# Four feed-forward stages whose operands share eight blocks of SBUF, first evictions that go to the result's place, and a reordered last column block

## The chip, the cores and the metric

The kernel runs on one core of a Trainium2 chip as one program. The metric is the device time of one execution in microseconds (us); three runs of the kernel before are shown. Engines are named as in the profile: PE is the matrix engine and PEld its weight loads, DVE the vector engine, ACT the scalar engine, POOL GpSimd, SP the engine that only issues transfers. A row such as "L298" names line 298 of the kernel before; the order listings of the changed kernel carry its own line numbers, about 20 higher.

## The reference, cut to what matters

Two blocks of two layers each work on x of 512 tokens by 1024 features in float32. Each layer has a mixer (forgetting attention, HGRN2, stick-breaking attention with pooling, gated linear attention) and then a feed-forward part of width 2816. The change touches the four feed-forward parts and the norms in front of them:

```python
def swiglu_ffn(h, w_in, w_out):                      # layers 0 and 1
    gate, up = jnp.split(jnp.einsum('bsd,df->bsf', h, w_in), 2, axis=-1)
    return jnp.einsum('bsf,fd->bsd', jax.nn.silu(gate) * up, w_out)

def conv_ffn(h, w_up, conv_w, conv_b, w_down):       # layers 2 and 3
    u = h @ w_up
    up = jnp.pad(u, ((0, 0), (CONV_WIDTH - 1, 0), (0, 0)))
    conv = conv_b
    for j in range(CONV_WIDTH):
        conv = conv + conv_w[j] * up[:, j:j + s]
    a, g = jnp.split(conv, 2, axis=-1)
    return (jax.nn.silu(a) * g) @ w_down
```

In front of each stands rms_norm(h, gain).

## The kernel before, in words

**Numbers.** A float32 operand is held as a high part (fp32r) and a low part; a product is three matmuls (`mm3`, L296). Making the parts is a "split": a cast on ACT and a subtraction on DVE (L148 and L149 for activations, L201 and L202 for weights).

**The up product.** The four feed-forward stages are called F0 to F3 here (`plan_up` tags up0 to up3). The product with w_up is a Winograd scheme over 2x2 quadrants: seven products p = 1 to 7 in place of eight, for each of 11 column blocks j of 256 columns of each half. The left operands of the seven (`LEFT`, L751) are made by `combine` (L415) from the normed activation: a11 and a12 from the first half of the tokens, then s1 = a22-a21, s4, s2, s3 = a11-a21 and a22. They lie in pool "xc" (L105), each 8 KB a partition. The sum y that `combine` works in lies above it in pool "y". The right operands are weights, loaded by SP into raw buffers, to which POOL adds other quadrants with accumulating transfers (L166, L204), and split into weight slots W0 to W3. So one raw buffer serves three products in turn: p5, then p6, then p4 (and p3, then p7), with an accumulating transfer between them.

**Order.** `up_order` (L677) sets PE's order: first (j, 1) and (j, 2) for j = 0 to 3 (`up_first`, run while the second half of the norm is still under way), then the rest. From j = 4 each block runs (j,5), (j+1,1), (j,3), (j,6), (j+1,2), (j,7), (j,4). A product is 24 matmuls of 256 columns. PE follows the program's order (`in_order`); DVE, ACT and POOL take the order that the Tile scheduler gives them, and each runs its own queue strictly in that order.

**Evictions.** p5 and then p3 accumulate in one PSUM bank z, and p6 and then p7 in the bank of p1. So p5 has to be copied out before p3 may add to z, and p6 before p7. `swiglu_evac` (L821) copies p5 to a temporary "p5" (L837) and p6 to "u" (L840) in pool "upt"; `conv_evac` (L855) copies them straight to hid (L878, L880), and for j = 0 and 1 POOL copies the gate half from its early buffer c to "g" (L876) in "upt". Pool "upt" lies where y lay.

**The down product.** hid (22 tiles of 512) is split into the resident region R of eight blocks, a tail, and, for tiles 0 and 1, the weight slot W3 (`hidden_at`, L665), and multiplied with w_down (`down`, L922; `out_gemm`, L520). R moves to the other side of SBUF in each feed-forward stage: `ffn_up` (L899) closes the old R, opens W3, hid and three more raw buffers there, and once the up product stands in the program closes xc and opens the new R over it.

A pool's tile that takes the place of an older tile waits for the older one's last use. `high_priority` tells the scheduler to place instructions ahead of others that are ready.

## Time and profile before

| | us |
|---|---|
| median of 3 runs | 2666.98 (2663.35 to 2672.43) |
| the profiled execution, its own time | 2667.84 |
| span of its instructions | 2666.1 |
| PE busy | 2502.1 (94%) |
| DVE busy | 1516.6 (57%) |
| ACT busy | 1173.9 (44%) |
| POOL busy | 660.9 (25%) |
| mean granted TensorE clock | 0.972 of full |

Busy shares are averages over the whole program. PE is the engine that is nearly always busy, so what can be saved is read from its idle time, place by place. A granted clock of 1.00 is 2.4 GHz and 0.50 is 1.2 GHz; a stretch with a mean in between held both.

### The profile page before, as it was taken

To read this page: it belongs to the slowest core of one execution; us is meant where nothing else is said; L and a number is where in the kernel's file an instruction comes from. 1 tells how busy PE (TensorE), PEld (TensorE's weight loads), DVE (VectorE), ACT (ScalarE), POOL (GpSimd) and SP (SyncE) were. 2 spreads that over 40 slices of the span, in tenths; PEclk is the share of its full clock that TensorE was granted. 3 is DMA by queue.
4 is the path that set the end of the run, shared out by engine and by line. 5 is a ranking of instruction groups with operands and counts; after the bars stand their busy time and mean duration, and the time that the engine had idled before them with its cause. 6 is when DMAs were issued, how large, how long until landed. Compare 5 with 4: busy or idle time off the path is not lost. (4 is left out here: it accounts for less than half of the span.)

```text
span 2666.1 us, 40655 instructions
## 1 busy us (share of the span) xinstructions
PE 2502.1 (94%) x16381; PEld 2219.3 (83%) x16381; DVE 1516.6 (57%) x2338; ACT 1173.9 (44%) x1920; POOL 660.9 (25%) x578
## 2 busy tenths in 40 slices
PE   8999889999999998999998998799899999889899
PEld 6677889988898988999897678799687778889778
DVE  5666565552555556655526766677623445677741
ACT  4445445543232234554424543565523333456541
POOL 0000243311321114333024124354112001444300
PEclk9999999999999999999999999899899999999999
DMA  4223279953122124998322116788331224778531
GB/s 131 74 66 100 72 147 191 173 119 123 48 66 70 56 80 111 182 182 159 123 80 71 56 56 132 154 171 150 98 111 50 64 72 130 152 150 171 121 123 40
DMA packets 302776, 294.92 MB, mean 111 GB/s; under 512 B 11581, under 2 KB 292763, under 8 KB 302587
## 3 DMA queue, kind: packets, MB, share of 16 engines
q1 hardware_dynamic: 208123, 195.47, 23.7%
q0 software_dynamic: 94384, 96.81, 23.5%
q8 instruction: 129, 2.11, 0.3%
q14 instruction: 60, 0.49, 0.1%
q10 hardware_dynamic: 80, 0.03, 0.0%
HBM read 290.15 MB, written 2.13 MB: 110 GB/s over the span
## 5 line engine op out<-in xcount | busy, mean ns | idle before, releaser
L202 DVE TENSOR_TENSOR W<-raw,W 128x1024 fp32r<-128x1024 f32 x436 | 551.6, 1269 | 504.6 <-ACT W L201 501.0
L201 ACT CAST W<-raw 128x1024 fp32r<-128x1024 f32 x455 | 472.3, 1041 | 657.3 <-PE g L298 315.0
L298 PE MATMUL g<-R,W 128*128 128x512 f32 (+2 forms) x3096 | 696.5, 373 | 16.5 <-ACT R L148 15.0
L298 PEld LDWEIGHTS g<-R,W 128*128 128x128 f32 (+1 forms) x3096 | 512.9, 191 | 109.5 <-ACT R L148 16.5
L298 PE MATMUL g<-s,W 128*128 128x256 f32 x3840 | 492.4, 288 | 69.5 <-ACT hid L878 22.3
L298 PEld LDWEIGHTS g<-s,W 128*128 128x128 f32 x3840 | 479.9, 195 | 75.4 <-ACT hid L878 25.3
L298 PE MATMUL g<-W,R 128*128 128x256 f32 (+1 forms) x1224 | 235.1, 338 | 0.0
L298 PEld LDWEIGHTS g<-W,R 128*128 128x128 f32 x1224 | 182.1, 192 | 25.9 <-issue 7.4
L298 PE MATMUL a<-a,W 128*128 128x256 f32 x1536 | 197.8, 285 | 0.3 <-POOL a L149 0.3
L298 PEld LDWEIGHTS a<-a,W 128*128 128x128 f32 x1536 | 190.4, 191 | 0.4 <-POOL a L149 0.4
L204 POOL DMA_DIRECT2D raw<-in_ffn_w_in_dram x80 | 106.5, 1374 | 206.4 <-DVE W L202 198.2
L204 POOL DMA_DIRECT2D raw<-in_ffn_w_up_dram x80 | 109.0, 1493 | 88.4 <-DVE W L202 80.7
L298 PE MATMUL g<-a,W 128*128 128x256 f32 x864 | 111.5, 285 | 4.2 <-DVE a L149 4.2
L298 PEld LDWEIGHTS g<-a,W 128*128 128x128 f32 x864 | 107.2, 192 | 5.1 <-DVE a L149 5.1
L298 PE MATMUL g<-R,R 128*128 128x256 f32 (+1 forms) x792 | 105.3, 288 | 0.7 <-ACT y L596 0.7
L298 PEld LDWEIGHTS g<-R,R 128*128 128x128 f32 x792 | 99.4, 192 | 2.7 <-ACT y L596 1.1
L895 POOL TENSOR_TENSOR hid<-u,s 128x512 f32<-128x512 f32 x44 | 70.3, 1608 | 121.9 <-ACT s L892 114.2
L298 PE MATMUL g<-R,X 128*128 128x256 f32 (+1 forms) x528 | 94.0, 333 | 0.0
L202 DVE TENSOR_TENSOR X<-raw,X 128x1024 fp32r<-128x1024 f32 (+1 forms) x39 | 41.1, 1060 | 85.2 <-ACT X L201 85.2
L298 PEld LDWEIGHTS g<-R,X 128*128 128x128 f32 x528 | 80.6, 190 | 9.8
L201 ACT CAST X<-raw 128x1024 fp32r<-128x1024 f32 (+1 forms) x46 | 42.8, 937 | 100.6 <-PE g L298 72.5
L355 POOL TENSOR_TENSOR acc<-acc,sq 128x512 f32<-128x512 f32 x19 | 28.2, 1483 | 233.2 <-ACT sq L354 233.0
(404 smaller groups left out, 3539.0 us busy)
## 6 DMA issues: line engine op xcount, KB each, us to landing
raw<-in_ffn_w_in_dram POOLq DMA_DIRECT2D x88, 512.0 KB, 6.1
raw<-in_ffn_w_up_dram POOLq DMA_DIRECT2D x88, 512.0 KB, 6.3
raw<-in_ffn_w_in_dram SPq DMA_DIRECT2D x74, 512.0 KB, 4.6
raw<-in_ffn_w_up_dram SPq DMA_DIRECT2D x74, 512.0 KB, 4.4
raw<-in_ffn_w_out_dram SPq DMA_DIRECT2D x40, 512.0 KB, 3.5
raw<-in_ffn_w_down_dram SPq DMA_DIRECT2D x40, 512.0 KB, 3.6
raw<-in_hgrn_w_in_dram SPq DMA_DIRECT2D x32, 512.0 KB, 4.1
raw<-in_fox_w_in_dram SPq DMA_DIRECT2D x24, 512.0 KB, 3.8
```

What stands on the lines that cost most here:

```text
L201: nc.scalar.copy(hi, raw)
L202: (nc.gpsimd if s.early else nc.vector).tensor_sub(lo, raw, hi.bitcast(F32))
L204: nc.gpsimd.dma_start(raw.rearrange("p (k c) -> p k c", k=s.nk), s.add, accum_op=ALU.add)
L298: self.nc.tensor.matmul(*args, **kw, **(dict(skip_group_check=True) if skip else {}))
L355: eng.tensor_add(acc[:, cols], acc[:, cols], sq[:, :n])
L895: nc.gpsimd.tensor_mul(hid[:, t], u, s)
```

## The change

1. **Blocks.** One pool of eight blocks of 8 KB stands on a side; its tenants take a block one after the other. On the side of xc, block 0 holds the first half of y (ya), then W3, then R0; blocks 1 to 7 hold a11, a12, s1, s4, s2, s3, a22, then R1 to R7. The second half of y (yb) stands above. hid starts where W3 stood. `hidden_at` fills R in the order 1, 2, 3, 4, 0, 5, 6, 7, and the tail holds six tiles in place of four; W3 no longer holds hid's first two.
2. **Evictions.** `swiglu_evac` copies p5 and p6 to their place in hid; z is added in a step of its own (p == 3) once p3 and p6 are both done. The gate's part for j = 0 and 1 moves from p5 to p7.
3. **combine** runs at high priority, and its POOL steps (two or four L149, two L450) go to DVE.
4. **Order.** The last seven products of blocks 9 and 10 are reordered, and the last (10, 7) gets a load and an accumulating transfer of its own.

```diff
+        self.open_blocks(self.other_side())
+        pool, close = self.open_pool("y", self.other_side())
+        y = Rows(self.blocks(0, "ya", [P, 4, S], F32), pool.tile([P, 4, S], F32, tag="yb", name="yb"))
+        self.xc = {n: self.blocks(1 + i, n) for i, n in enumerate(("a11", "a12", "s1", "s4", "s2", "s3", "a22"))}
...
-            self.combine(pool, work, half, gain, R)
+            with self.tc.high_priority(400):
+                self.combine(pool, work, half, gain, R)
...
-            nc.gpsimd.tensor_sub(a21[i], a11[i], a21[i])
-        for i in range(2):
+            nc.vector.tensor_sub(a21[i], a11[i], a21[i])
             put("s3", g[i], a21[i])
         for i in range(2):
-            put("a22", g[i], a22[i], nc.gpsimd)
+            put("a22", g[i], a22[i])
...
-        if t < 2:
-            return self.slot_at["W3"], t
-        if t >= 18:
-            return self.tail, t - 18
-        k = t - 2 if self.r_side == "left" else t % 16
-        return self.R[k // 2], k % 2
+        if t >= 16:
+            return self.tail, t - 16
+        return self.R[(1, 2, 3, 4, 0, 5, 6, 7)[t // 2]], t % 2
...
+        y, z = n - 2, n - 1
+        rest += [(y, 5), (z, 1), (y, 3), (y, 6), (z, 2), (z, 5), (y, 7), (y, 4), (z, 6), (z, 3), (z, 7), (z, 4)]
...
             elif p == 5:
-                kept[j, "p5"] = new("p5")
-                nc.scalar.copy(kept[j, "p5"], ps)
+                nc.scalar.copy(out[1], two(ps))
             elif p == 6:
-                u = new("u")
-                nc.scalar.copy(u, ps)
-                nc.vector.tensor_add(u, other, u)
-                nc.vector.tensor_mul(out[0], two(u), two(kept.pop((j, "g"))))
+                nc.scalar.copy(out[0], two(ps))
+            elif p == 3:
+                nc.vector.tensor_add(out[0], two(ps), out[0])
...
-        wp, self.close_w3 = self.open_pool("w3", side)
-        self.slot_at["W3"] = wp.tile([P, 2048], F32R, tag="W3", name="W3")
+        self.slot_at["W3"] = self.blocks(0, "W3")
```

Three places show how the instructions move. **POOL at the start of F2** (names with in_ffn_w_up_dram are accumulating transfers; raw_92 and raw_93 serve (0, 5) and (1, 5), the next two numbers above 14900 (before) or 14850 (now) (2, 5) and (3, 5)). Before:

```order
L166 DMA raw_93<-in_ffn_w_up_dram 128x4x256
L367 TENSOR_TENSOR r<-v,mhalf 128x2
L149 TENSOR_TENSOR a_14198<-y,a_14198 128x2x256 x2
L204 DMA raw_92<-in_ffn_w_up_dram 128x4x256
L450 TENSOR_TENSOR y<-y 128x2x256 x2
L876 COPY g<-c_14730 128x2x256
L876 COPY g<-c_14783 128x2x256
L166 DMA raw_14909<-in_ffn_w_up_dram 128x4x256
L204 DMA raw_93<-in_ffn_w_up_dram 128x4x256
L166 DMA raw_14910<-in_ffn_w_up_dram 128x4x256
L204 DMA raw_14908<-in_ffn_w_up_dram 128x4x256
```

Now:

```order
L186 DMA raw_93<-in_ffn_w_up_dram 128x4x256
L387 TENSOR_TENSOR r<-v,mhalf 128x2
L224 DMA raw_92<-in_ffn_w_up_dram 128x4x256
L186 DMA raw_14851<-in_ffn_w_up_dram 128x4x256
L186 DMA raw_14852<-in_ffn_w_up_dram 128x4x256
L224 DMA raw_93<-in_ffn_w_up_dram 128x4x256
L224 DMA raw_14850<-in_ffn_w_up_dram 128x4x256
L901 COPY g<-c_14675 128x2x256
L901 COPY g<-c_14728 128x2x256
L224 DMA raw_91<-in_ffn_w_up_dram 128x4x256
L224 DMA raw_92<-in_ffn_w_up_dram 128x4x256
```

The four POOL steps of combine are gone, and four transfers now stand ahead of the two copies of g instead of behind them.

**DVE at the start of F2**, from the weight split of (0, 5) on (in the change L464 and L467 are the sums, L473 is a11-a21, L169 the low half of an activation's split, L222 that of a weight). Before:

```order
L202 TENSOR_TENSOR W_90<-raw_92,W_90 128x1024
L441 TENSOR_TENSOR sums<-y 128x512 x2
L779 TENSOR_TENSOR c_14783<-a,c_14783 128x512
L149 TENSOR_TENSOR s_14194<-sums,s_14194 128x2x256 x2
L444 TENSOR_TENSOR sums<-sums,y 128x512 x2
L149 TENSOR_TENSOR s_14197<-y,s_14197 128x2x256
L445 TENSOR_TENSOR y<-sums,y 128x2x256 x2
L152 SCALAR_TENSOR_TENSOR s_14195<-sums,s_14195 128x2x256
L149 TENSOR_TENSOR s_14197<-y,s_14197 128x2x256
L152 SCALAR_TENSOR_TENSOR s_14195<-sums,s_14195 128x2x256
L149 TENSOR_TENSOR s_14196<-y,s_14196 128x2x256 x2
L202 TENSOR_TENSOR W_88<-raw_93,W_88 128x1024
```

Now:

```order
L222 TENSOR_TENSOR W_90<-raw_92,W_90 128x1024
L464 TENSOR_TENSOR sums<-yb,ya 128x512
L169 TENSOR_TENSOR a_14147<-yb,a_14147 128x2x256
L464 TENSOR_TENSOR sums<-yb,ya 128x512
L169 TENSOR_TENSOR a_14147<-yb,a_14147 128x2x256
L473 TENSOR_TENSOR ya<-ya 128x2x256
L802 TENSOR_TENSOR c_14728<-a,c_14728 128x512
L169 TENSOR_TENSOR s_14143<-sums,s_14143 128x2x256
L473 TENSOR_TENSOR ya<-ya 128x2x256
L169 TENSOR_TENSOR s_14143<-sums,s_14143 128x2x256
L169 TENSOR_TENSOR s_14146<-ya,s_14146 128x2x256
L467 TENSOR_TENSOR sums<-sums,ya 128x512 x2
```

DVE has the two splits of a22 and the two differences a11-a21 in addition, and no weight split stands among them.

**PE at the end of F2's up product**: a11 to a22 and s1 to s4 are the left operands (14194 before and 14143 now is s1), g<-R and g<-W_14900,W the down product. Before:

```order
L298 MATMUL g<-s_14197,W_89 128x256 x24
L298 MATMUL a<-a_14198,W_14900 128x256 x24
L298 MATMUL g<-s_14194,W_90 128x256 x24
L298 MATMUL g<-s_14196,W_88 128x256 x24
L298 MATMUL g<-s_14195,W_89 128x256 x24
L298 MATMUL g<-s_14197,W_90 128x256 x24
L298 MATMUL a<-a_14198,W_88 128x256 x24
L298 MATMUL g<-W_14900,W_89 128x512 x12
L298 MATMUL g<-R_17143,W_89 128x512 x12
L298 MATMUL g<-R_17144,W_90 128x512 x12
```

Now:

```order
L318 MATMUL g<-s_14143,W_89 128x256 x24
L318 MATMUL g<-s_14146,W_14842 128x256 x24
L318 MATMUL a<-a_14147,W_90 128x256 x24
L318 MATMUL g<-s_14145,W_88 128x256 x24
L318 MATMUL g<-s_14144,W_89 128x256 x24
L318 MATMUL g<-s_14146,W_90 128x256 x24
L318 MATMUL a<-a_14147,W_88 128x256 x24
L318 MATMUL g<-R_17078,W_89 128x512 x12
L318 MATMUL g<-R_17079,W_89 128x512 x12
L318 MATMUL g<-R_17080,W_90 128x512 x12
```

(10, 5) has moved up by two products, (10, 6) stands ahead of (10, 3), and the down product begins from R and not from W3. **DVE there**, before:

```order
L863 SCALAR_TENSOR_TENSOR s<-g,ccol,s 128x511
L864 SCALAR_TENSOR_TENSOR u<-hid,ccol,u 128x510
L863 SCALAR_TENSOR_TENSOR s<-g,ccol,s 128x511
L864 SCALAR_TENSOR_TENSOR s<-g,ccol,s 128x510 x2
L149 TENSOR_TENSOR R_17143<-hid,R_17143 128x2x256 x2
L149 TENSOR_TENSOR R_17144<-hid,R_17144 128x2x256 x2
L149 TENSOR_TENSOR R_17145<-hid,R_17145 128x2x256 x2
```

Now:

```order
L222 TENSOR_TENSOR W_88<-raw_91,W_88 128x1024
L169 TENSOR_TENSOR R_17079<-hid,R_17079 128x2x256 x2
L222 TENSOR_TENSOR W_89<-raw_93,W_89 128x1024
L169 TENSOR_TENSOR R_17080<-hid,R_17080 128x2x256 x2
L169 TENSOR_TENSOR R_17077<-hid,R_17077 128x2x256 x2
L913 TENSOR_TENSOR g<-a,g 128x2x256
L888 SCALAR_TENSOR_TENSOR u<-hid,ccol,u 128x511 x2
L889 SCALAR_TENSOR_TENSOR u<-hid,ccol,u 128x510
L222 TENSOR_TENSOR W_90<-raw_14852,W_90 128x1024
L889 SCALAR_TENSOR_TENSOR u<-hid,ccol,u 128x510
```

The splits of hid into R, which stood behind the whole convolution (L863 and L864), now stand among the last weight splits.

## Rows read from the trace of the kernel before

**Rows 1.** Waits of PE, whole span: who for whom, us in total, times, longest.

```profile
PE g L298 <- ACT hid L878: 22.3, 15, 4.5
PE g L298 <- ACT R L148: 19.6, 7, 6.2
PE g L298 <- ACT hid L880: 18.7, 4, 7.9
```

**Rows 2.** By stretch: length, busy PE, PEld, DVE, ACT, POOL, clock, DMA share; F0, F1.

```profile
356.00:381.00 25.00, 16.55 (x102) 16.14 (x101) 17.23 (x20) 11.25 (x18) 13.07 (x9) 0.80 0.92 143
552.00:576.00 24.00, 19.66 (x142) 18.06 (x142) 14.48 (x18) 13.32 (x20) 3.06 (x2) 1.00 0.58 140
1062.00:1087.00 25.00, 16.51 (x113) 16.11 (x112) 17.44 (x21) 12.48 (x19) 13.19 (x9) 0.86 0.91 141
1257.00:1282.00 25.00, 20.66 (x139) 19.14 (x139) 14.07 (x18) 12.90 (x19) 3.06 (x2) 0.93 0.55 134
```

**Rows 3.** The same view, start and end of F2 and of F3.

```profile
1642.00:1683.00 41.00, 29.12 (x201) 28.09 (x200) 19.07 (x22) 15.69 (x21) 15.96 (x10) 0.83 0.74 143
...
1864.00:1902.00 38.00, 26.00 (x150) 23.22 (x149) 26.91 (x35) 23.10 (x36) 8.76 (x7) 0.82 0.39 93
2298.00:2324.00 26.00, 15.09 (x105) 14.47 (x105) 10.88 (x10) 11.13 (x14) 6.73 (x5) 0.80 0.96 193
...
2500.00:2538.00 38.00, 25.74 (x157) 23.03 (x157) 27.48 (x35) 23.00 (x36) 9.40 (x7) 0.87 0.42 96
```

**Rows 4.** The same view: the steady middle of F0's up product.

```profile
400.00:500.00 100.00, 100.00 (x844) 100.00 (x843) 57.70 (x60) 51.39 (x65) 34.42 (x25) 1.00 0.97 185
```

**Rows 5.** Timeline of PE at F0's start: start, us, what, idle before and releaser.

```profile
360.65 7.36 PE L298 MATMUL m<-s,W 128*128 128x256 f32 x47 [4.15 <-DVE s L149]
372.30 8.72 PE L298 MATMUL m<-s,W 128*128 128x256 f32 x48 [4.29 <-ACT p L837]
```

**Rows 6.** Timeline of DVE there.

```profile
352.74 1.74 DVE L441 TENSOR_TENSOR sums<-y 128x512 f32<-128x512 f32 x2
...
370.94 0.68 DVE L149 TENSOR_TENSOR s<-y,s 128x512 fp32r<-128x512 f32 x1
```

**Rows 7.** Timeline of PE at F2's start.

```profile
1649.17 11.21 PE L298 MATMUL m<-s,W 128*128 128x256 f32 x70 [2.05 <-DVE W L202]
...
1675.27 7.61 PE L298 MATMUL g<-s,W 128*128 128x256 f32 x48 [7.81 <-ACT hid L880]
...
1712.09 8.15 PE L298 MATMUL g<-s,W 128*128 128x256 f32 x50 [8.35 <-ACT g L873]
```

**Rows 8.** Timeline of POOL there.

```profile
1648.13 5.42 POOL L876 COPY g<-c 128x512 f32<-128x512 f32 x2 [7.34 <-DVE s L149]
```

**Rows 9.** Timeline of ACT there.

```profile
1673.69 1.04 ACT L201 CAST W<-raw 128x1024 fp32r<-128x1024 f32 x1 [1.64 <-DMA raw<-in_ffn_w_up_dram]
1674.64 0.58 ACT L880 COPY hid<-g 128x512 f32<-128x512 f32 x1
```

**Rows 10.** Timeline of DVE there.

```profile
1634.06 3.49 DVE L441 TENSOR_TENSOR sums<-y 128x512 f32<-128x512 f32 x2
...
1641.88 1.28 DVE L444 TENSOR_TENSOR sums<-sums,y 128x512 f32<-128x512 f32 x2
...
1647.90 4.62 DVE L202 TENSOR_TENSOR W<-raw,W 128x1024 fp32r<-128x1024 f32 x4
```

**Rows 11.** Timeline of PE at the end of F2's up product.

```profile
1871.46 8.38 PE L298 MATMUL g<-s,W 128*128 128x256 f32 x48 [4.29 <-ACT hid L878]
...
1896.30 19.00 PE L298 MATMUL g<-R,W 128*128 128x512 f32 x71 [6.21 <-ACT R L148]
```

**Rows 12.** Timeline of ACT there.

```profile
1895.65 8.41 ACT L148 CAST R<-hid 128x512 fp32r<-128x512 f32 x16
```

**Rows 13.** The page, DMA queues: packets, MB, share of 16 engines' span.

```profile
q1 hardware_dynamic: 208123, 195.47, 23.7%
q0 software_dynamic: 94384, 96.81, 23.5%
```

More of the change, by code (lines that the diff above doesn't have):

```diff
@@ L36, in backwards, with __init__, __getitem__ @@
     return bass.AP(ap.tensor, ap.offset + (n - 1) * step, rest + [(-step, n)])
+class Rows:
+    def __init__(self, *parts):
+        self.parts = parts
+    def __getitem__(self, key):
+        p, c, cols = key
+        if isinstance(c, int):
+            return self.parts[c // 4][p, c % 4, cols]
+        return self.parts[c.start // 4][p, c.start % 4 : c.start % 4 + c.stop - c.start, cols]
 class Chunk:
@@ L92, in open_pool, with open_blocks @@
         return pool.__enter__(), lambda: pool.__exit__(None, None, None)
+    def open_blocks(self, side):
+        pool, self.close_next = self.open_pool("blocks", side)
+        self.blocks = lambda i, name, shape=[P, 2048], dt=F32R: pool.tile(shape, dt, tag=f"b{i}", name=name, bufs=1)
     def open_r(self, side):
-        pool, self.close_r = self.open_pool("rreg", side)
-        self.R = [pool.tile([P, 2048], F32R, tag=f"R{i}", name=f"R{i}") for i in range(8)]
-        self.r_side = side
+        self.R = [self.blocks(i, f"R{i}") for i in range(8)]
+        self.close_r, self.r_side = self.close_next, side
         for i in range(8):
@@ L105, in open_xc @@
     def open_xc(self):
-        pool, self.close_xc = self.open_pool("xc", self.other_side())
-        self.xc = {n: pool.tile([P, 2048], F32R, tag=n, name=n) for n in ("a11", "a12", "s1", "s2", "s4", "s3", "a22")}
+        self.open_blocks(self.other_side())
+        pool, close = self.open_pool("y", self.other_side())
+        y = Rows(self.blocks(0, "ya", [P, 4, S], F32), pool.tile([P, 4, S], F32, tag="yb", name="yb"))
+        self.xc = {n: self.blocks(1 + i, n) for i, n in enumerate(("a11", "a12", "s1", "s4", "s2", "s3", "a22"))}
+        return pool, y, close
     def open_e(self, side):
@@ L429, in combine @@
         if not half:
+            norm(0)
             for c in range(NC):
-                norm(c)
-                put("a12" if c >= 4 else "a11", c % 4, work[:, c, cols], nc.gpsimd if c in (4, 6) else None, 1)
+                if c < NC - 1:
+                    norm(c + 1)
+                put("a12" if c >= 4 else "a11", c % 4, work[:, c, cols], None, 1)
             return
@@ L686, in up_order @@
             rest += o
[L687 to L689 removed]
+        for j in range(E, n - 2):
+            rest += [(j, 5), (j + 1, 1), (j, 3), (j, 6), (j + 1, 2), (j, 7), (j, 4)]
+        y, z = n - 2, n - 1
+        rest += [(y, 5), (z, 1), (y, 3), (y, 6), (z, 2), (z, 5), (y, 7), (y, 4), (z, 6), (z, 3), (z, 7), (z, 4)]
         return first, rest
@@ L705, in spec @@
         def spec(j, p, raw, **kw):
-            slots = early if (j, p) in first else W[:3] if (j, p) in rest[-3:] else W
+            slots = early[j > 0] if (j, p) in first else W[:3] if (j, p) in rest[-3:] else W
             self.specs.append(Spec(tag, 4, 256, slots, j == 0 and p < 3, raw, **kw))
@@ L742, in plan_up @@
                 c[j] = load(j, 1, 1)
-                spec(j, p, c[j], loads=[c[j]], add=src(j, 0, 1))
+                last = j == NF // 2 - 1
+                spec(j, p, c[j], loads=[c[j]], add=None if last else src(j, 0, 1), ends=[c[j]] if last else [])
+                if last:
+                    c[j] = load(j, 1, 1, src(j, 0, 1))
             elif p == 6:
@@ L746, in plan_up @@
             elif p == 7:
-                spec(j, p, c[j], ends=[c[j]])
+                spec(j, p, c[j], loads=[c[j]], ends=[c[j]])
             else:
@@ L779, in c11, with up @@
         self.nc.vector.tensor_add(out, y, out)
-    def up(self, tag, st, evac, hid):
-        x, y, z = st["x"], st["y"], {}
+    def up(self, tag, st, evac):
+        x, y, z, done = st["x"], st["y"], {}, set()
         rest = self.up_order()[1]
         for j, p in rest:
-            if p == 5 and j < self.EARLY:
+            if p == (7 if j in st["c11"] else 5) and j < self.EARLY:
                 evac(j, 2, x[j], y.get(j), st["c11"].get(j))
@@ L811, in up @@
                 evac(j, p, v)
-            if (j, p) == rest[-3]:
-                self.occupy("W3")
-                for t in range(2):
-                    self.split(self.halves(hid[:, t]), self.hid(t, 0, "F"), self.hid(t, 1, "F"))
+            done.add((j, p))
+            if p in (3, 6) and {(j, 3), (j, 6)} <= done:
+                evac(j, 3, z.pop(j))
     @staticmethod
@@ L845, in evac @@
                 nc.scalar.copy(u, ps)
-                nc.gpsimd.tensor_add(kept[j, "p5"], kept[j, "p5"], u)
+                nc.gpsimd.tensor_add(out[1], out[1], two(u))
             else:
@@ L850, in evac @@
                 nc.scalar.activation(u, u, AF.Silu)
-                nc.vector.tensor_mul(out[1], two(kept.pop((j, "p5"))), two(u))
+                nc.vector.tensor_mul(out[1], out[1], two(u))
         return evac
@@ L880, in evac @@
                 nc.scalar.copy(a[:, :, lo], two(ps))
-                nc.vector.tensor_add(a[:, :, lo], two(other), a[:, :, lo])
+            elif p == 3:
+                nc.vector.tensor_add(a[:, :, lo], two(ps), a[:, :, lo])
             elif p == 7:
@@ L1962, in two_blocks_kernel @@
     CV = None
+    net.open_blocks("left")
     net.open_r("left")
```

29 lines of the change are left out of this document (13 added, 16 removed).

## Prediction

> **What bounds the kernel now.** The waits of PE, summed by who ended them, come first. The largest are for ACT's copies of products into hid (22.3 and 18.7 us) and for ACT's splits into R (19.6 us) [rows 1]. All three are evictions or operand splits of the feed-forward stages. Next I read the busy time by stretch, to see where such waits lie. In the middle of an up product PE has no idle time at all: 844 matmuls in 100 us at clock 1.00 [rows 4], so a product of 24 takes 2.84 us, and two take 5.7 us. The start and the end of the up product look different. PE is idle there for length less busy time: 8.45 and 4.34 us in F0, 8.49 and 4.34 in F1 [rows 2], 11.88 and 12.0 in F2, 10.91 and 12.26 in F3 [rows 3]. That is 72.7 us at eight places. The granted clock in them is 0.80 to 1.00; it falls to the half level (1.2 GHz) after PE has stood idle, so each wait costs more than its own length: 48 matmuls took 8.72 us after F0's second wait [rows 5] instead of 5.7. The reader should see that the kernel is bound by PE, and that only these eight places can give time back.
>
> The timelines then tell what is late. At F0's start PE waits for s1's split, and then again until ACT has copied p5 out of PSUM (372.30) [rows 5]. That copy could run only after the last split that reads y, 370.94 + 0.68 us [rows 6], since its temporary lies on y's place. At F2's start the same kind of wait holds POOL: the copies of g wait 7.34 us for the same split and then take 5.42 us [rows 8], and the accumulating transfers behind them in POOL's queue start late. ACT's weight cast then waits for such a transfer, and the copy of p6 that PE needs stands behind that cast (1673.69, then 1674.64) [rows 9]; PE is idle for 7.81 us [rows 7]. At the end, p3 follows p5 and p7 follows p6 at once, so PE waits out the copy between them (4.29 us), and the splits into R begin only behind the whole convolution (6.21 us) [rows 11].
>
> **The parts, one by one.** PE's matmuls are the same in number; 24 at each stage's end change places. All terms are therefore waits.
>
> *Start of F0.* A DVE step of 128x512 takes 0.64 us when POOL is quiet (1.28 for two), a weight split 1.15 (4.62 for four) [rows 10]. From the end of the norms at 352.7 [rows 6] the changed order has eight such steps and one weight split up to s1's splits: 6.3 us. The first of the two is enough to start, so PE goes on at about 358.8 instead of 360.65 [rows 5]. From there to s4's first split stand eight more steps and three weight splits, 8.6 us: 367.5, and PE at 367.9 instead of 372.30. No copy waits for y any more, since p5 goes to hid, on the other side of SBUF. Two products later PE is at 373.6, against 381.0 [rows 5]. Both waits still exist (2.5 and 3.4 us), so I leave one short stretch at the half clock, 1.7 us, as in F1's end (25 us at 0.93) [rows 2]. Gain 5.7. *F1* is the same place, but the clock there was 0.86 and not 0.80 [rows 2], so 1.5 less is to be had: 4.2.
>
> *Start of F2.* The two sums took 3.49 us beside POOL's steps, two of the same size 1.28 us without them [rows 10]. With POOL's steps gone and four put on DVE, 18 steps stand between 1634.1 and the weights of (1, 5): 11.5 us and 1.15 for the split, so 1646.7 against 1649.17 [rows 7]. The transfers for (2, 5) and (3, 5) now stand ahead of POOL's copies of g, and so do those for (1, 6) and (0, 7). One accumulating transfer of 0.52 MB takes 3.4 us (96.81 MB in 23.5% of the span), a plain load 1.7 [rows 13]; DMA was 0.74 busy in this stretch [rows 3], so there is room. Five products at 2.84 us bring PE from 1646.9 to (0, 7) at 1661.1. I add 1.2 us, because ACT's copy of p6 still stands behind a cast that waits for a transfer, and 5.7 for two products: 1668.0 against 1682.9 [rows 7]. Less 1.7 for the clock and 1.0 for the norm ahead, where DVE does two splits that POOL did: gain 12.2. *F3* has 10.91 us idle and a clock of 0.80 [rows 3]. Part of that half clock lay inside the idle time, so I count 2 of it, and keep 2 for short waits: 11.0.
>
> *After that*, PE's wait of 8.35 us in F2 for the copy of g [rows 7] (F3 has its twin) stays. DVE's order of convolution steps in front of that copy is unchanged, and the chain starts from products of the same spacing.
>
> *End of F0 and F1.* Idle 4.34 us each [rows 2], from the pairs (10,5)-(10,3) and (10,6)-(10,7) and the first split into R. Now two products lie between the first pair and one between the second, more than a copy of 0.58 us [rows 9] and a cast of 1.04 ahead of it need. I keep 0.5 in each: 3.8, and in F1 with its clock of 0.93 (1.5) 5.3.
>
> *End of F2 and F3.* Idle 12.0 and 12.26 us [rows 3]. The splits into R (16 casts in 8.41 us) [rows 12] now run while PE still has products, so the down product can start at once. Of the half clock, 4 and 3 us come back (38 us at 0.82 and 0.87 [rows 3], less what lay inside idle time). Against it: these splits put 16 steps, 10.2 us, on DVE among the last weight splits. By my count along DVE's new order the first weights of the down product come 1 us late, and I leave 1.7 us for the clock. Gains 13.3 and 12.6.
>
> *The rest.* One more load in each stage (1.7 us) lies beside PE. A copy into hid instead of a temporary has the same size. The blocks themselves add no instruction; the waits that they add are W3's for ya and each R for its operand, and both tenants are done before the split stands next on ACT and DVE, by the changed order.
>
> On the transfers: DMA is busy for a share of 0.97 in the steady stretch while PE is never idle [rows 4], so the transfers keep up with PE at its full rate. The Trainium skill (SBUF — State Buffer, "A bandwidth-pool intuition that's wrong (but worth ruling out)") says that HBM is almost always the end-to-end bottleneck. By that rule the gains at the eight places would return as waits for transfers, and the sum would be near 0; the trace does not agree for this kernel's steady stretch, with 0 us idle.
>
> Sum: 5.7 + 3.8 + 4.2 + 5.3 + 12.2 + 13.3 + 11.0 + 12.6 = 68.1 us. The profiled execution took 2667.84, so 2599.7; it lies 0.9 above the median shown, and I take **2599** for a median.
>
> **The rivals.**
>
> *Transfers catch up with PE.* A late block needs three loads and four accumulating transfers, 5.1 + 13.6 = 18.7 us [rows 13], and PE's seven products take 19.9. That is little slack, and the four early blocks need one more load each. If PE, no longer held up, runs into casts that wait for transfers, about half of the sum goes: 2667.8 - 34 = 2634. For it: ACT waited for a transfer at 1673.69 [rows 9]. Against it: the steady stretch, and shares of 0.39 and 0.42 at the ends [rows 3].
>
> *The first evictions still wait.* hid lies over the whole old R, as one tile; if its first write waits for something late there, or the copies of g hold POOL as before, the starts give nothing and only the ends remain: 68.1 - 33.1 = 35.0, so 2633. Against it: the early weights in R are used up before s1 is needed.
>
> *The starts' second waits go too.* If the waits at 1712.09 [rows 7] and its twin vanish, 16.7 us and some clock more: 2579.
>
> *Slower: splits into R block the weight splits.* Each split into a block waits for the last product that reads the block's operand, and DVE and ACT queue strictly. If it stands ahead of a weight split that the next product needs, PE waits for two casts, two splits and one weight cast and split, 1.05 + 1.3 + 1.04 + 1.15 = 4.5 us [rows 9, 10, 12]. Eight blocks in four stages make 32 x 4.5 = 145 us: 2599 + 145 = 2744. Half of that is enough to pass 2667. It decides itself by the distance: in the changed order three products lie between (10, 2), which frees a12, and (10, 3), whose weights stand behind that split, so DVE would have to run 8.5 us behind PE. At the end of F2 it is busy 26.9 of 38 us [rows 3], which leaves some room.
>
> **How the numbers follow.** The forecast has 0.6, transfers 0.14, evictions that still wait 0.10, the further gain 0.07, the slower case 0.06; 0.03 is left for the unforeseen. A measurement of this kernel can tell about 0.3% (8 us) from no change. The range reaches from 2578 (the further gain) to 2640 (the two cases in which half is lost, with some margin); it leaves out the slower case and the remainder. Faster by over 0.3%: 0.60 + 0.07 and nearly all of 0.24, 0.89. Within: 0.04. Slower: 0.07.
>
> **What would show it.** In the new profile F0's and F1's starts should have two waits, under 3.5 us each, and no wait of p3 for ACT's copy of p5. In F2 and F3 the transfers for (2, 5) should be issued ahead of the copies of g, and PE should come to (0, 7) some 14 us sooner after the norm; the wait of about 8 us for g should still be there. At the ends PE should go from (10, 4) into the down product with under 2 us idle. The waits for splits into R should all but vanish from PE's list. I am wrong if these places still show over half of their idle time, if PE waits for weight splits at the ends, or if the steady stretches, now without idle time, show waits for weights.

## The result and the profile after

The changed kernel takes 2604.12 us (median of 4 runs, 2602.27 to 2606.96); the kernel before, on the same chip, 2669.03. The ratio is 0.976, with a 95% interval of 0.9739 to 0.9781. The prediction was 2599, with a range of 2578 to 2640.

The profiled execution took 2605.56 us, 62.3 less than the one before it was compared with (2667.84). The page of the changed kernel says where it comes from: its span is 2603.8, and

```profile
PE 2483.0 (95%) x16381; PEld 2205.1 (85%) x16381; DVE 1514.3 (58%) x2362; ACT 1173.5 (45%) x1920; POOL 628.3 (24%) x554
```

PE was idle for 2666.1 - 2502.1 = 164.0 us before and is for 120.8 now: 43.2 less. It also needs 19.1 us less for the same 16381 recorded matmuls, which goes with the clock: the mean granted clock rose from 0.972 to 0.981. The waits of PE in the changed kernel, summed by who ended them (total, times, longest):

```profile
PE g L318 <- ACT g L898: 17.2, 2, 8.9
...
PE g L318 <- ACT hid L903: 12.6, 13, 1.9
PE g L318 <- ACT hid L860: 7.7, 2, 4.1
...
PE g L318 <- ACT R L168: 6.9, 5, 3.2
```

Against [rows 1], the waits for p6's copy (L880, now L905) are gone from the head of the list, and those for splits into R fell from 19.6 to 6.9 us; what is left of these lies in the mixers. The first row is the copy of g that was expected to stay (8.35 and 8.89 us). The third row is p5's copy in F0 and F1, at a new place: before, PE waited for it at the starts (8.7 us) and the ends (4.3 us) of these stages, and now it waits in the blocks ahead of the ends.

The eight places by stretch, in the columns of [rows 2]: F0's start, its late blocks, its end; the same for F1; then F2's start and end and F3's.

```profile
354.50:379.50 25.00, 20.07 (x152) 19.47 (x151) 19.10 (x26) 15.15 (x23) 6.42 (x5) 0.93 0.86 144
510.00:536.50 26.50, 22.40 (x189) 22.19 (x187) 11.63 (x13) 11.35 (x16) 7.83 (x7) 1.00 0.87 166
545.00:569.00 24.00, 24.00 (x194) 23.54 (x193) 20.49 (x27) 18.07 (x28) 6.15 (x3) 1.00 0.48 125
1058.00:1083.00 25.00, 19.96 (x150) 19.07 (x150) 19.39 (x26) 15.12 (x22) 6.57 (x6) 0.93 1.02 166
1215.00:1241.00 26.00, 22.37 (x185) 22.17 (x184) 12.31 (x13) 11.32 (x15) 7.55 (x6) 0.97 0.92 175
1250.00:1275.00 25.00, 25.00 (x199) 24.32 (x198) 21.78 (x28) 18.66 (x29) 5.86 (x3) 1.00 0.47 127
1636.00:1677.00 41.00, 38.88 (x328) 38.67 (x327) 29.96 (x35) 24.01 (x31) 16.91 (x13) 1.00 0.96 177
1840.00:1878.00 38.00, 35.76 (x231) 32.09 (x230) 36.10 (x44) 26.73 (x40) 11.70 (x7) 1.00 0.38 108
2248.00:2274.00 26.00, 23.05 (x182) 22.84 (x181) 11.13 (x11) 10.99 (x16) 7.79 (x7) 0.93 0.99 196
2450.00:2488.00 38.00, 35.78 (x212) 31.54 (x211) 35.48 (x44) 25.67 (x40) 12.09 (x7) 0.96 0.42 117
```

PE's idle time is length less busy time. It fell from 8.45 to 4.93 us at F0's start, from 11.88 to 2.12 at F2's, from 12.0 to 2.24 at F2's end [rows 2, 3]. The very ends of F0 and F1 have none. But two stretches that had no part in the prediction, the late blocks of F0 and F1 (8 to 10, ahead of the ends), now have 4.10 and 3.63.

The gain of each place can be read by pairing the k-th recorded matmul of both traces, and taking how much earlier it starts behind a place than ahead of it:

| place | forecast us | measured us |
|---|---|---|
| F0 start, end | 5.7, 3.8 | 6.0, -0.7 |
| F1 start, end | 4.2, 5.3 | 4.4, 0.05 |
| F2 start, end | 12.2, 13.3 | 15.1, 14.9 |
| F3 start, end | 11.0, 12.6 | 9.1, 12.3 |
| sum | 68.1 | 61.1 |

The ends of F0 and F1 stand here together with the late blocks in front of them. Alone the ends gained 5.0 and 6.6 us; the late blocks lost 5.8 and 6.5.

Between the places 0.9 us remain on balance, with larger parts of both signs: the mixers behind F0 and F1 gave back 3.0 and 2.8 us, that behind F2 gained 5.0. The last one is a matter of the clock and is shown in the last section.

**F0's start** in the changed kernel, PE's timeline:

```profile
358.68 5.85 PE L318 MATMUL m<-s,W 128*128 128x256 f32 x47 [1.73 <-DVE s L169]
365.69 0.38 PE L318 MATMUL m<-s,W 128*128 128x256 f32 x1 [1.16 <-ACT s L168]
368.11 7.38 PE L318 MATMUL m<-s,W 128*128 128x256 f32 x47 [2.03 <-DVE s L169]
```

The waits stand where they were counted to be, at 358.68 (forecast 358.8) and 368.11 (367.9), where [rows 5] have 360.65 and 372.30.

**F0's late blocks**, PE, ACT and POOL:

```profile
536.50 7.38 PE L318 MATMUL g<-s,W 128*128 128x256 f32 x48 [4.10 <-ACT hid L860]
```

```profile
533.46 1.04 ACT L221 CAST W<-raw 128x1024 fp32r<-128x1024 f32 x1 [8.10 <-DMA raw<-in_ffn_w_in_dram]
...
535.88 0.58 ACT L860 COPY hid<-g 128x512 f32<-128x512 f32 x1
```

```profile
524.57 1.28 POOL L186 DMA_DIRECT2D raw<-in_ffn_w_in_dram  x1 [13.66 <-DVE W L222]
525.33 3.15 POOL L224 DMA_DIRECT2D raw<-in_ffn_w_in_dram  x2
```

the transfer of the kernel before that answers to the first one behind L186, and the cast that waits for it there:

```profile
526.33 1.28 POOL L204 DMA_DIRECT2D raw<-in_ffn_w_in_dram  x1 [10.01 <-DVE W L202]
```

```profile
532.81 1.05 ACT L201 CAST W<-raw 128x1024 fp32r<-128x1024 f32 x1 [1.92 <-DMA raw<-in_ffn_w_in_dram]
```

and two stretches of the changed kernel, in the columns of [rows 2]:

```profile
523.00:526.00 3.00, 3.00 (x28) 3.00 (x27) 2.29 (x3) 1.66 (x3) 1.43 (x2) 1.00 0.04 12
528.00:536.50 8.50, 4.40 (x38) 4.19 (x36) 2.65 (x4) 3.04 (x5) 3.49 (x4) 0.99 1.23 194
```

The chain, in order. L186 is the accumulating transfer of the extra load for (10, 7), which is the last-but-one product of the stage. Accumulating transfers are no more than before (96.81 MB in both); (10, 7)'s has moved forward, onto a buffer of its own, and one plain load a stage has come with it (195.47 MB before, 197.57 now). It stands in POOL's queue ahead of transfers that block 9 needs, and waits until its raw buffer is free and loaded. The transfer behind it went at 526.33 in the kernel before; less the 5.53 us by which PE is ahead now, it was due at 520.8, and it went at 525.33, 4.5 us late. Just before, from 523 to 526, the DMA engines moved next to nothing (a share of 0.04); from 528 on, the transfers that had been held run together (1.23, against 0.97 in the steady stretch [rows 4]; this share can pass 1). The cast on ACT that needs the data comes at 533.46. By the same reckoning it was due at 527.3 (532.81 before), so it is 6.2 us late: 4.5 from the queue, and 1.7 because it starts 8.1 us behind the issue and not 6.5, with one transfer more just ahead. So that weight cast waits 8.10 us for data, p5's copy stands behind the cast, and PE waits 4.10 us for the copy and then runs 48 matmuls in 7.38 us instead of 5.7. That is 5.8 us, as much as F0's start had won.

**F2's start**, PE, ACT and POOL:

```profile
1649.77 3.13 PE L318 MATMUL m<-s,W 128*128 128x256 f32 x24 [2.12 <-ACT hid L903]
...
1693.52 3.73 PE L318 MATMUL g<-s,W 128*128 128x256 f32 x17 [8.35 <-ACT g L898]
```

```profile
1648.18 1.04 ACT L221 CAST W<-raw 128x1024 fp32r<-128x1024 f32 x1 [4.48 <-DMA raw<-in_ffn_w_up_dram]
```

```profile
1642.25 2.58 POOL L224 DMA_DIRECT2D raw<-in_ffn_w_up_dram  x2 [7.74 <-DVE W L222]
1643.98 2.85 POOL L901 COPY g<-c 128x512 f32<-128x512 f32 x2
```

The copies of g take 2.85 us and wait for nothing, where they waited 7.34 and took 5.42 [rows 8], and the transfers are issued ahead of them. Of 11.88 us of waits 2.12 are left.

**F2's end**, PE: the down product starts and then waits once, for a weight split.

```profile
1861.26 21.02 PE L318 MATMUL g<-R,W 128*128 128x512 f32 x89 [2.24 <-DVE W L222]
```

### The profile page after: what moved, and what is told of

Same layout as the page of the kernel before. It is cut to its first block, busy times and chain, and to the rows that moved or that the text cites. A ratio compares the mean times of both kernels' runs of the same rounds, so it can differ in the third digit from the quotient of the medians.

```text
span 2603.8 us, 40615 instructions
## 1 busy us (share of the span) xinstructions
PE 2483.0 (95%) x16381; PEld 2205.1 (85%) x16381; DVE 1514.3 (58%) x2362; ACT 1173.5 (45%) x1920; POOL 628.3 (24%) x554
## 3 DMA queue, kind: packets, MB, share of 16 engines
q1 hardware_dynamic: 210235, 197.57, 24.4%
q0 software_dynamic: 94384, 96.81, 23.9%
## 4 chain that ended last, share of the span: by engine, by line
PE 78%; DVE 8%; DMA 5%; issue 4%; ACT 3%; POOL 1%; ACTq 0%; SPq 0%; POOLq 0%; DVEq 0%
PE g L318 60%; PE a L318 7%; PE m L318 3%; DMA raw<-in_ffn_w_up_dram 3%; DMA raw<-in_ffn_w_in_dram 2%; DVE W L222 2%; ACT W L221 1%; PE a L1391 1%; PE m L1391 1%; PE a L1433 1%; PE m L1832 1%; ACT s L887 1%; DVE sums L419 1%; PE g L1186 0%; DVE R L222 0%
## 5 line engine op out<-in xcount | busy, mean ns | idle before, releaser
L222 DVE TENSOR_TENSOR W<-raw,W 128x1024 fp32r<-128x1024 f32 x436 | 547.6, 1259 | 439.7 <-ACT W L221 432.6
L318 PE MATMUL g<-s,W 128*128 128x256 f32 x3840 | 482.5, 286 | 37.6 <-ACT g L898 17.2
L318 PEld LDWEIGHTS g<-s,W 128*128 128x128 f32 x3840 | 472.6, 193 | 41.1 <-ACT g L898 17.7
L921 POOL TENSOR_TENSOR hid<-u,s 128x512 f32<-128x512 f32 x44 | 80.3, 1835 | 124.5 <-ACT s L918 116.7
L222 DVE TENSOR_TENSOR X<-raw,X 128x1024 fp32r<-128x1024 f32 (+1 forms) x39 | 41.1, 1061 | 84.2 <-ACT X L221 84.2
L318 PE MATMUL g<-tail,X 128*128 128x512 f32 (+1 forms) x384 | 80.7, 367 | 0.0
```

The source lines that it names most:

```text
L222: (nc.gpsimd if s.early else nc.vector).tensor_sub(lo, raw, hi.bitcast(F32))
L318: self.nc.tensor.matmul(*args, **kw, **(dict(skip_group_check=True) if skip else {}))
L921: nc.gpsimd.tensor_mul(hid[:, t], u, s)
```

## Experiments

They were run in three rounds, each on one chip together with the kernel before, whose median was 2665 to 2667 us in them. "The change" stands for 2604.1 us; it was run only with the result, where the kernel before took 2669.0. So a difference from the change is good to some 4 us, and what is smaller is read from the traces, by pairing matmuls.

### The end of the up product: order and blocks

**Order undone** (e4_oldorder).

```diff
-        for j in range(E, n - 2):
-            rest += [(j, 5), (j + 1, 1), (j, 3), (j, 6), (j + 1, 2), (j, 7), (j, 4)]
-        y, z = n - 2, n - 1
-        rest += [(y, 5), (z, 1), (y, 3), (y, 6), (z, 2), (z, 5), (y, 7), (y, 4), (z, 6), (z, 3), (z, 7), (z, 4)]
+        for j in range(E, n):
+            o = [(j, 5), (j + 1, 1), (j, 3), (j, 6), (j + 1, 2), (j, 7), (j, 4)]
+            rest += [x for x in o if x[0] < n]
...
-                last = j == NF // 2 - 1
+                last = False
```

Expected: 

> The changed kernel with the order of the kernel before in the last blocks (and so without the extra load). Theory A: in F2 and F3 the two waits between p5 and p3 and between p6 and p7 return (4.3 + 1.5 us, with the half clock about 8 each), while the early splits into R stay; in F0 and F1 the old waits of 2.2 + 1.5 us return, about 4 with the clock, and the new ones (5.8 and 6.5) go: 2604 + 16 - 4 = 2616 (2608 to 2622). Rival B: the reorder made the whole gain at the ends of F2 and F3 (15 and 12 us): 2604 + 27 - 4 = 2627. Rival C: the new waits of F0 and F1 come from the splits into R and stay: 2604 + 16 + 8 = 2628, with those waits in the trace.

Measured: 2615.4 us (2611.6 to 2621.6). PE's timeline at F0's end and at F2's:

```profile
549.95 7.47 PE L318 MATMUL g<-s,W 128*128 128x256 f32 x48 [2.17 <-ACT hid L859]
558.97 3.12 PE L318 MATMUL g<-s,W 128*128 128x256 f32 x24 [1.55 <-ACT hid L861]
...
1850.32 8.00 PE L318 MATMUL g<-s,W 128*128 128x256 f32 x48 [5.18 <-ACT hid L902]
1859.82 3.12 PE L318 MATMUL g<-s,W 128*128 128x256 f32 x24 [1.50 <-ACT hid L904]
```

Theory A holds, in size too: the pairs p5-p3 and p6-p7 wait again, F2 loses 6.7 us and F3 5.7. In F0 the new wait at 536.5 is gone and the two old ones are back, with 0.1 us between the two orders; in F1 the old one is 0.7 better. So the reorder, with its extra load, is worth some 12 us in F2 and F3, and nothing in F0 and F1.

**The blocks filled the other way round** (e11_lateblocks).

```diff
-        return self.R[(1, 2, 3, 4, 0, 5, 6, 7)[t // 2]], t % 2
+        return self.R[(7, 6, 5, 0, 4, 3, 2, 1)[t // 2]], t % 2
```

Expected: 

> The changed kernel with the tiles of hid put into the blocks the other way round: tiles 0 and 1 go to the block of a22, which the very last product (10, 4) frees, and the blocks that are free early hold the last tiles. Theory A (the early splits, block by block, gave about half of the gain at the ends of F2 and F3): the down product waits for casts and splits behind the last product again, 4 to 9 us with the clock in each of F2 and F3, 2 to 4 in F0 and F1: 2604 + 18 = 2622 (2612 to 2628). Rival B: the order of the products made the gain alone: 2602 to 2608.

Measured: 2632.1 us (2628.3 to 2636.2), more than either theory said. PE at F2's end:

```profile
1873.21 0.50 PE L318 MATMUL g<-R,W 128*128 128x512 f32 x1 [2.68 <-ACT R L168]
1880.20 10.09 PE L318 MATMUL g<-R,W 128*128 128x512 f32 x33 [6.49 <-DVE R L169]
```

By the pairing of matmuls the ends of F2 and F3 lose 9.3 and 8.1 us, as theory A had it, but F0 and F1 lose 6.1 and 6.0, not 2 to 4: the down product meets one late split after the other. So the splits have to go first into the blocks that are free first. With the order (6.7 and 5.7 us) that is 16.0 and 13.8 us, a little more than the 14.9 and 12.3 gained at the ends of F2 and F3. It is no exact division: this run turns the filling round and does not bring back the old place of R, which was not tried.

### Why the ends of F0 and F1 gained nothing

**The extra transfer later in POOL's queue** (e1_late).

```diff
+            ok = self.after.get(key)
-            name = next((n for n in self.raw_free if extra or n in self.RAWS), None)
+            name = next((n for n in self.raw_free if (extra or n in self.RAWS) and (ok is None or self.was.get(ok) == n)), None)
...
                     c[j] = load(j, 1, 1, src(j, 0, 1))
+                    self.after[c[j]] = k2
```

Expected: 

> The changed kernel, but the extra load of the last (10, 7) takes the raw buffer that (10, 2) frees, so that its accumulating transfer stands four transfers later in POOL's queue. Theory A (the transfer, early in POOL's queue, holds up the next two, which block 9 needs): the new waits of PE for p5's copy at the end of F0 (4.10 us) and F1 (3.63 us) go, with the half clock behind them; the lag to the kernel before fell by 5.8 and 6.5 us there, so 2604 - 12 = 2592 us, down to 2 us less if (10, 7) itself now comes late. Rival B (one more load and accumulating transfer are too much for the DMA engines at that point, or the splits into R keep DVE from the weight splits): both waits stay above 3 us and the time is 2602 to 2606.

Measured: 2605.2 us (2602.5 to 2608.9). The time is what theory B said, but the trace is not: the wait of block 9 is gone with its 5.8 us, and two waits stand later, in the last products of block 10. PE, ACT and POOL (its L187 is the extra transfer):

```profile
548.69 5.72 PE L320 MATMUL g<-s,W 128*128 128x256 f32 x46 [0.75 <-DVE W L223]
557.39 4.49 PE L320 MATMUL g<-s,W 128*128 128x256 f32 x24 [2.98 <-ACT hid L865]
```

```profile
546.33 1.05 ACT L222 CAST W<-raw 128x1024 fp32r<-128x1024 f32 x1 [8.85 <-DMA raw<-in_ffn_w_in_dram]
```

```profile
535.97 1.28 POOL L187 DMA_DIRECT2D raw<-in_ffn_w_in_dram  x1 [7.27 <-DVE W L223]
536.72 1.84 POOL L225 DMA_DIRECT2D raw<-in_ffn_w_in_dram  x1
```

The transfer now holds up the next one, which (10, 6) needs: that cast is the one that waits 8.85 us. At both places that were tried, the transfer on a buffer of its own makes some product late. How much of it is here the wait in POOL's queue and how much the transfer's own time was not told apart.

**No extra transfer** (e9_order2): an order in which every raw buffer is used again as many products later as in the steady blocks.

```diff
-        rest += [..., (z, 5), (y, 7), (y, 4), (z, 6), (z, 3), (z, 7), (z, 4)]
+        rest += [..., (z, 5), (y, 7), (z, 3), (z, 6), (y, 4), (z, 7), (z, 4)]
...
-                last = j == NF // 2 - 1
+                last = False
```

Expected: 

> The changed kernel with another order of its last seven products: (10, 5), (9, 7), (10, 3), (10, 6), (9, 4), (10, 7), (10, 4). Each product stands as far behind the one whose raw buffer it uses again as in the steady blocks, so the extra load and accumulating transfer go. Theory D (e1_late lost elsewhere what it won, because the DMA engines are full there and the extra 0.52 + 0.52 MB cost their time wherever they stand): nothing is late any more at the end of F0 and F1, 5.8 and 6.5 us come back: 2604 - 12 = 2592 (2588 to 2596); F2 and F3 as they were. Rival B (the end of F0 and F1 loses because copies out of PSUM stand behind casts on ACT in any such order): 3 to 5 us of waits for L860 or L862 stay in each, 2598 to 2606.

Measured: 2594.0 us (2588.2 to 2596.0), 10 less than the change. PE runs through F0's late blocks and its end without a wait:

```profile
532.32 5.88 PE L318 MATMUL g<-s,W 128*128 128x256 f32 x48
538.03 3.01 PE L318 MATMUL a<-a,W 128*128 128x256 f32 x24
540.87 11.58 PE L318 MATMUL g<-s,W 128*128 128x256 f32 x96
```

F0 gives 5.8 us more than the change and F1 6.5. So the loss comes with the extra load and its early transfer. That splits into R or copies behind casts make it in any order falls. Of theory D the result came, but not its reason. The accumulating transfers are as many with the extra load as without it, so only 0.52 MB a stage are extra, and not twice that; and the engines stood at 0.04 while POOL's queue was held, and were full only behind that. In the trace of the change the queue is the larger part (4.5 of 6.2 us). No run takes the load away and leaves the order as it is, so the two were separated by reading alone.

### What made the starts faster

**combine's steps back on POOL** (e5_pool).

```diff
-            nc.vector.tensor_sub(a21[i], a11[i], a21[i])
+            nc.gpsimd.tensor_sub(a21[i], a11[i], a21[i])
...
-            put("a22", g[i], a22[i])
+            put("a22", g[i], a22[i], nc.gpsimd)
```

(and the splits of columns 4 and 6, likewise.)

Expected: 

> The changed kernel with the steps of combine that the change moved to DVE put back on POOL. Theory A: at the starts of F2 and F3 the copies of g stand ahead of the transfers for (2, 5) and (3, 5) again and wait for the sums, so 8 to 12 us return in each; in F0 and F1 the sums run beside POOL and take longer, about 2 us each: 2604 + 24 = 2628 (2618 to 2635). Rival B: high priority and the place of the evictions made the starts faster, and POOL's steps hardly matter: 2602 to 2610.

Measured: 2635.9 us (2628.2 to 2638.4), theory A. F2's start, DVE, POOL and PE:

```profile
1630.24 3.49 DVE L464 TENSOR_TENSOR sums<-yb,ya 128x512 f32<-128x512 f32 x2
...
1634.26 4.34 DVE L169 TENSOR_TENSOR s<-sums,s 128x512 fp32r<-128x512 f32 x2
```

```profile
1645.04 4.60 POOL L901 COPY g<-c 128x512 f32<-128x512 f32 x1 [7.00 <-DVE s L169]
1649.59 1.30 POOL L186 DMA_DIRECT2D raw<-in_ffn_w_up_dram  x1
```

```profile
1671.32 7.84 PE L318 MATMUL g<-s,W 128*128 128x256 f32 x48 [7.73 <-ACT hid L905]
```

The chain of the kernel before is back whole: slow sums, a copy of g that waits 7.00 us, transfers behind it, PE's wait of 7.73 for p6's copy [rows 7 to 10]. F2's start loses 14.9 of its 15.1 us and F3's 7.9 of 9.1. F0's and F1's lose 2.5 and 1.8, and their late blocks, where PE then waits less, give 2.7 and 1.1 back. The trace is of the fastest of six executions and holds 22.7 of the 31.8 us between the medians; the rest was not traced. The run does not say how much of the chain is POOL's order and how much the slow sums that hold its copy.

**No high priority** (e6_noprio).

```diff
-            with self.tc.high_priority(400):
-                self.combine(pool, work, half, gain, R)
+            self.combine(pool, work, half, gain, R)
```

Expected: 

> The changed kernel without high priority for combine. Theory A: weight splits (1.15 us each) stand among the sums on DVE again, three or four of them ahead of s1's and s4's splits, so each of the four starts loses 3 to 4 us: 2604 + 14 = 2618 (2610 to 2626). Rival B: with the four POOL steps on DVE the order follows from the data, and priority moves little: 2602 to 2607.

Measured: 2605.6 us (2602.4 to 2609.9): rival B. F0's start has the same waits to 0.01 us, and for a good reason: on DVE, ACT and POOL the scheduler's order at all four starts is the same with and without the priority. So the priority changed nothing here.

**Temporaries for p5 and p6** (e7_temps).

```diff
             elif p == 5:
-                nc.scalar.copy(out[1], two(ps))
+                kept[j, "p5"] = new("p5")
+                nc.scalar.copy(kept[j, "p5"], ps)
             elif p == 6:
-                nc.scalar.copy(out[0], two(ps))
+                kept[j, "u"] = new("u")
+                nc.scalar.copy(kept[j, "u"], ps)
```

Expected: 

> The changed kernel with p5 and p6 of F0 and F1 copied to temporaries in upt, as in the kernel before, and not to hid. Theory A: the temporary of p5 lies on yb again, so its copy waits for the last split that reads yb, and PE for the copy, about 4 us with 1 of half clock in each of F0 and F1: 2604 + 10 = 2614 (2608 to 2618), F2 and F3 as they were. Rival B: the sums are now so early that yb has been read when p5 is there: 2602 to 2607.

Measured: 2602.8 us (2600.3 to 2605.3): rival B, though not quite by its reason. F0's start, PE:

```profile
366.37 0.38 PE L318 MATMUL m<-s,W 128*128 128x256 f32 x1 [2.63 <-ACT p L861]
367.32 7.40 PE L318 MATMUL m<-s,W 128*128 128x256 f32 x47 [0.57 <-DVE s L169]
```

PE does wait for p5's copy again, 2.63 us; but then only 0.57 for s4's split, and 2.63 + 0.57 = 3.20 is what 1.16 + 2.03 is in the changed kernel. The split sets the time; the place of the eviction does not. In F1 the wait for the copy is 5.94 us, but PE had come 2.4 us earlier out of the norm, and behind it stands no later than without the edit.

**The gate with p5 again** (e8_gate5).

```diff
-            if p == (7 if j in st["c11"] else 5) and j < self.EARLY:
+            if p == 5 and j < self.EARLY:
```

Expected: 

> The changed kernel with the gate's part of blocks 0 and 1 evicted with p5 again and not with p7. Theory A: with the four POOL steps gone, POOL's order at the start of F2 and F3 is the same with it (four transfers ahead of the copies of g), so nothing is lost: 2602 to 2608. Rival B: the copies of g wait for the last split that reads the second half of y and hold the transfers behind them, 8 us in each of F2 and F3: 2620.

Measured: 2602.0 us (2598.6 to 2608.1): theory A. The orders of DVE, ACT and POOL are the same throughout.

**All three undone** (e12_three: the diffs of e5_pool, e6_noprio and e7_temps).

Expected: 

> The changed kernel with three parts undone at once: combine's steps on POOL (as in e5_pool), no high priority (e6_noprio), temporaries for p5 and p6 (e7_temps). Alone the last two cost nothing. Theory A: they stand in for each other, and together the starts of F0 and F1 go back to the kernel before, 2 to 4 us each more than in e5_pool: 2636 + 6 = 2642 (2638 to 2648). Rival B: what is left of the gain at the starts of F0 and F1 comes from the blocks and from the order of the sums: as e5_pool, 2628 to 2637.

Measured: 2634.9 us (2629.4 to 2637.4): rival B, the same as e5_pool. F0's and F1's starts lose 2.2 and 3.2 us of 6.0 and 4.4. What is left (3.8 and 1.2) must come from the rest of the change (two halves of y, the order of the norm's steps, the slots of the early weights); these weren't tried one by one. So most of F0's gain at its start has no shown cause. One thing the traces show: between the sums and s1's splits DVE had two weight splits in the kernel before (4.39 us beside POOL's steps) and has one in e5_pool (2.18 us).

### Beyond the change

**A third buffer of g** (e2_g3), and with it **the order of e9_order2** (e10_order2g3).

```diff
-                g = kept[j] = tp.tile([P, 2, S], F32, tag="g", name="g", bufs=2)
+                g = kept[j] = tp.tile([P, 2, S], F32, tag="g", name="g", bufs=3)
```

Expected of e2_g3: 

> The changed kernel with three buffers of g in place of two in the convolution stages. Theory A: the waits of PE for the copy of g in F2 (8.35 us) and F3 (8.89 us) are waits for a free buffer of g, whose last reader is the convolution of block 1; both go: 2604 - 17 = 2587, or 2583 with some half clock. Rival B: DVE and ACT are behind with the convolution there, whatever the buffers; then the wait moves to the next copy that PE needs, and less than 5 us is won: 2599 to 2604.

Measured: 2591.7 us (2589.3 to 2592.6), 12.5 less than the change, between the two theories. PE in F2, where the wait of 8.35 us stood:

```profile
1678.64 14.70 PE L318 MATMUL g<-s,W 128*128 128x256 f32 x120 [0.65 <-ACT hid L903]
...
1712.69 7.41 PE L318 MATMUL g<-s,W 128*128 128x256 f32 x48 [2.21 <-ACT hid L903]
```

Both waits are gone, so they were for a free buffer. F2 and F3 win 9.9 and 10.1 us there, but give back 1.8 and 4.5 in the blocks behind, where PE now meets ACT, which is still busy with the convolution.

Expected of e10_order2g3: 

> The order of e9_order2 and the three buffers of g of e2_g3 together. Theory A: they act at different places (ends of F0 and F1, starts of F2 and F3), so the gains add: 2604 - 12 - 12.5 = 2579.5 (2575 to 2584). Rival B: a faster start of F2 and F3 meets transfers that are not faster, and the end of those stages gives part back: 2585 to 2590.

Measured: 2574.6 us (2574.1 to 2576.1), a ratio of 0.966 to the kernel before (0.9647 to 0.9673): the gains add, and 5 us more than the 24.5 counted; where these lie was not followed up. This is the fastest version, about 1% below the change.

**p5's copy on DVE** (e14_dve), on top of that.

```diff
             elif p == 5:
-                nc.scalar.copy(a[:, :, hi], two(ps))
+                nc.vector.tensor_copy(a[:, :, hi], two(ps))
```

Expected: 

> The version of e10_order2g3 with p5 of F2 and F3 copied by DVE and not by ACT. In e10_order2g3 PE waits for that copy 12 times in F2 and F3, 20 us in all, and the copy stands behind four steps of the convolution and a weight cast on ACT; on DVE it stands behind two steps. Theory A: each wait is about 0.7 us shorter: 2574.6 - 8 = 2566 (2562 to 2570). Rival B: the copy makes the weight splits behind it on DVE late, and PE waits for those: 2572 to 2582.

Measured: 2576.6 us (2575.9 to 2577.7): rival B, nothing won. PE in F2:

```profile
1700.63 5.93 PE L318 MATMUL g<-s,W 128*128 128x256 f32 x48 [2.07 <-ACT W L221]
...
1712.22 4.63 PE L318 MATMUL g<-s,W 128*128 128x256 f32 x24 [2.82 <-ACT hid L905]
```

It is ACT's casts and p6's copies that come late now. So the engine of this one copy is not what is in the way; that the convolution's work is was not shown by a run.

## Why the prediction was right, and where not

**The sum.** 68.1 us were forecast at eight places and 61.1 came. Six places are within 3 us of their terms; two, the ends of F0 and F1, gave -0.7 and 0.05 instead of 3.8 and 5.3, and these 9.75 us are more than the whole difference. That the total came so near is in part luck: 2.9 and 1.6 us too much in F2 stand against 9.75 too little here.

**The step that failed** is "One more load in each stage (1.7 us) lies beside PE". The load was counted; that (10, 7)'s accumulating transfer moves forward in POOL's queue with it was not followed. There it waits for its load ahead of transfers that block 9 needs, and costs 5.8 and 6.5 us. In F2 and F3, where POOL's order puts it one transfer later, it hardly waits (0.48 us and not at all), and PE loses nothing in the late blocks. It isn't free there either: e9_order2 has no wait of 2.2 us at the start of the down product, gives most of that back elsewhere, and is some 1 us better in each of F2 and F3. The waits that the reorder was to remove did go, as forecast (4.34 to 0 us). e4_oldorder and e9_order2 show both halves. The distances were counted short by one, to the safe side: three products and not two lie between (10, 5) and (10, 3), and four and not three between (10, 2) and (10, 3).

**Starts of F0 and F1.** The count of DVE's steps was good to 0.2 us. One reason given beside it was not: "No copy waits for y any more, since p5 goes to hid" is true of the change but worth nothing, by e7_temps. The wait that counts is for s4's split: already before, its last one ended at 371.62, only 0.68 us ahead of PE's start behind the copy [rows 5, 6]. The mark set for being wrong, over half of the idle time left, is met here (4.93 of 8.45 us in F0), but the forecast itself left 5.9 us of waits there: the mark was badly chosen, the terms were good.

**Starts of F2 and F3.** The mechanism is right: POOL's four steps, the copies of g and the transfers behind them (e5_pool, 14.9 of 15.1 us in F2). The term for F2 was 3 us too small: the half clock and the wait for the weights of (1, 5) that it kept did not come, the granted clock is 1.00. In F3 it was 2 too large, since p5's copy waits for a cast there for 2.95 us.

**Ends of F2 and F3.** 14.9 and 12.3 for 13.3 and 12.6. PE's wait for the first weights of the down product is there too, 2.24 us in F2 and 2.22 in F3 where 1 was counted, over the 2 us that were named as the mark. It is a wait for a weight split, another of the marks for being wrong, though a small one.

**What was to stay** stayed: 8.35 and 8.89 us for g. The prediction gave no reason in terms of buffers; e2_g3 supplies it.

**The rivals.** Transfers did make PE wait in the late blocks of F0 and F1, mostly for a reason of POOL's queue, and a little at the starts of F2 and F3 (2.12 and 2.95 us, behind casts that wait 4.48 and 5.60 us for data). But no half of the sum went that way: at the starts the DMA share rose to 0.96 in F2 and 0.99 in F3 and the gains stayed. That the first evictions still wait, so that the starts give nothing, is refuted by the 34.6 us of the starts. The slower case (splits into R ahead of weight splits) did not show: PE waits for no weight split at the ends but those of 2.24 and 2.22 us. e11_lateblocks shows what late splits into R cost when the down product itself waits for them, 6 to 9 us a stage.

## What to carry to other kernels

Follow every added or moved transfer through the queue that issues it: here an accumulating one that waited for its buffer stopped those behind it, and cost PE time a block away from the product it serves. Before a load is added to break a chain, look for an order that keeps each buffer's reuse as far apart as in the steady state; here it was there and gave some 10 us. And when a place of eviction and a split are both late, find out which one is binding before the gain is credited to either.
